# A new order of the S5 mixer's steps, the skip added on TensorE, lags in the output's PSUM bank, three buffers for weight products

## The chip, the cores and the metric

The kernel runs on one core of a Trainium2 chip. The metric is the device time of one execution in microseconds (us). TensorE (PE in the profile) multiplies matrices, VectorE (DVE) and ScalarE (ACT) work elementwise, GpSimd (POOL) works elementwise on SBUF only, and SyncE (SP) issues the DMAs.

## What is computed

A two-layer trunk over 512 tokens of width 1024, in float32. The change lies in the first mixer, an S5 state-space layer over 64 groups of 16 channels with 64 complex states each:

```python
u = rms_norm(h, a_norm) @ w_in
a_bar = exp(lam * dt);  b_bar = ((a_bar - 1) / lam) * b        # per group
s[t] = a_bar * s[t-1] + b_bar @ u[t]                           # complex scan over 512 tokens
y = real(c @ s) + d_skip * u
g = gelu(y);  val, gate = split(g @ w_glu)
h = h + val * sigmoid(gate)
```

After it come a gated feed-forward layer, stick-breaking attention and a second feed-forward layer. The change does not touch them.

## The kernel before

**Tiling.** Every large product is cut into a rounded high part and a residue, and three fp32r matmuls replace one (`mm3`, line 248). The 64 groups are worked through in four quarters `q`, each in two halves. Tokens are cut into 64 steps of L = 8, so the sum over the states becomes a short convolution inside a step of 8 (the "lags") and a recurrence over the 64 steps (the "states").

**Steps of a half (q, half).** Each is a method of the class `S5`, and the tuple `ORDER` (line 762) lists them by name.
- `turn`: eight PE transposes of the projected input into bank 2, one ACT copy to `u`.
- `weights`: six DVE operations (two complex products of 128x512), in the helper lines 836 and 837 (multiply) and 838 (add), to the tiles `w1`. `turn_weights`: eight transposes of `w1` into banks 3, then 2, two ACT copies to `vl`.
- `lags`: 16 small matmuls of `w1` with c. ACT copies most of the result to `ktt` (line 1198), and one DVE operation writes the last 16 columns with the skip `d_skip` added (line 1200). `turn_lags`: one transpose of `ktt`, an ACT copy to `kt`. `toeplitz`: eight DMAs of `kt` into `tz`.
- `outs`: six POOL operations and four DMAs, which fill `w2`.
- `inject`: 32 matmuls of `u` with `vl` into banks 4 and 5.
- `rotations` (once a quarter): six operations of 128x512 to the table `tab`, on DVE for q = 0 and 1, on POOL for q = 2 and 3. `states` (once a quarter): sixteen DVE operations with two scans, from banks 4 and 5 to `s`.
- `output`: 32 matmuls of `tz` and `u`, `w2` and `s` into bank 6, then a gelu on ACT in two parts. `turn_output`: eight transposes into bank 3, then `split_one` (lines 164 and 165): ACT writes the high part, DVE the residue. Bank 3 is free after the residue.

**Filler.** A plain number in `ORDER` takes that many steps of the generator `filler` (line 1376). It first projects quarters 1, 2 and 3 (16 steps each, six matmuls a step, called fills below), reads each projection on ACT (`read`), and then runs the first pass of the gated product (`first_pass`, three matmuls of 512 columns a fill). The fills left over when `ORDER` ends run after it, so a fill that is used early is missing later.

**What sets the order.** The calls run in the order of the tuple. On PE that order is kept (`manual_schedule(engines={PE})`, line 1437). On DVE, ACT, POOL and SP a planner decides at build time: it takes the instructions by the order of the program, and what is not ready by its own timeline lets later ones go first. The result is a fixed order for each queue. `START` (line 744) is an order by hand for PE, ACT and DVE in the part before, in which quarter 0 is projected.

**Buffers.** The temporaries of the complex products and of `states` on DVE are two tags, `tt1` and `tt2`, two buffers each (`tmp`, line 1148). `w1` has two buffers per part, `tab` has one. `LAG_BANKS` gives the PSUM banks of `lags` and `turn_lags`.

Of the kernel before, what the change touches and what calls it, by code (L numbers as in the profile page):

```python
# [7 lines left out]
F32 = mybir.dt.float32  # L8
# [3 lines left out]
ALU = mybir.AluOpType  # L12
PSUM = bass.MemoryType.PSUM

P = 128
T = 512
D = 1024
DC = D // P
# [676 lines left out]
def attention(e, ws, grow, r4=None):  # L695
# [31 lines left out]
L = 8  # L727
# [16 lines left out]
START = (  # L744
# [8 lines left out]
ST_BANK = 6  # L753
EXP_BANK = 7
G_BANK = 7
LAG_BANKS = ((1, 1), (3, 6), (3, 6), (3, 6))
P_BANKS = ((0, 1), (6, 0), (0, 1), (0, 1))
BC_BANKS = (4, 5, 4, 5)
X_BANKS = (2, 3, 4, 5, 6, 7, 2, 3)
GLU_POOL = (True, False)  # L760

ORDER = (
# [14 lines left out]
)  # L777


# [10 lines left out]
def flat(t):  # L790
    n = len(t.shape) - 1
    names = "abcd"[:n]
    return t.rearrange(f"p {' '.join(names)} -> p ({' '.join(names)})")
# [47 lines left out]
def cmul(*args):  # L841
    run(cmul_steps(*args))
# [18 lines left out]
class S5:  # L861
# [73 lines left out]
    def gains(self):  # L935
        e, nc = self.e, self.nc
        ps = e.bank(6)
        nc.tensor.transpose(ps[:, 0 : 2 * DC], self.nrow, e.ident[0 : 2 * DC, 0 : 2 * DC])
        self.gain = self.t([P, 2 * DC], F32, "gain")
        nc.vector.tensor_copy(self.gain, ps[:, 0 : 2 * DC])  # L940
        self.xhi, self.xlo, self.xps = [], [], []

    def turn_x(self, d):
# [184 lines left out]
    def read(self, q):  # L1128

        reg = self.reg  # L1130
        up = self.up[q] = self.t([C, 16, L, 16], F32, "up")
        for j in range(L):
            i, k = j % 4, j // 4
            pp = slice(C * k, C * k + C)
            self.nc.scalar.activation(
                up[:, :, j], reg[i][pp].rearrange("p (g h) -> p g h", h=16), AF.Copy, scale=self.r4[pp, i : i + 1])
# [14 lines left out]
    def weights(self, q, half):  # L1151

        W = [P, 4, L, 16]
        w1 = self.w1[q, half] = [self.t(W, F32, f"w1{k}", 2) for k in range(2)]
        sl = slice(8 * q + 4 * half, 8 * q + 4 * half + 4)
        gb = [g[:, :, sl].rearrange("p l q -> p q l").unsqueeze(3).broadcast_to(W) for g in (self.gre, self.gim)]
        bb = [b[:, sl].unsqueeze(2).broadcast_to(W) for b in self.b]
        cmul(self.nc.vector, self.tmp(W), w1[0], w1[1], gb, bb)
        for g in range(2):
            pp = slice(64 * g, 64 * g + 64)  # L1160
            for k in range(2):
                self.nc.scalar.copy(self.cm[half][k][pp, :, g], self.c[k][pp, sl])
# [22 lines left out]
    def lags(self, q, half):  # L1185

        e, nc = self.e, self.nc
        w1 = self.w1.pop((q, half))
        sl = slice(8 * q + 4 * half, 8 * q + 4 * half + 4)
        cm = self.cm[half]  # L1190
        ps = e.bank(LAG_BANKS[q][half])
        for k in range(2):
            for i in range(4):
                nc.tensor.matmul(
                    ps[32 * i : 32 * i + 32, 0:P], flat(cm[k][:, i]), flat(w1[k][:, i]), start=k == 0, stop=k == 1,
                    skip_group_check=True)
        ktt = self.ktt[q, half] = self.t([P, P], F32, "ktt", 2)
        nc.scalar.copy(ktt[:, 0 : P - 16], ps[:, 0 : P - 16])
        d = DC + 2 * q + half
        nc.vector.scalar_tensor_tensor(  # L1200
            out=ktt[:, P - 16 :], in0=self.eye, scalar=self.gain[:, d : d + 1], in1=ps[:, P - 16 : P], op0=ALU.mult, op1=ALU.add)

    def turn_lags(self, q, half):

        e, nc = self.e, self.nc
        ps = e.bank(LAG_BANKS[q][half])
        nc.tensor.transpose(ps[:, 0:P], self.ktt.pop((q, half)), e.ident)
# [130 lines left out]
    def store(self, d):  # L1338

        if d < 2:  # L1340
            if d == 0:
                self.p0 = self.t([P, 4, T], F32, "up")
            return [self.p0[:, 2 * d], self.p0[:, 2 * d + 1]]
        if d < 4:
            t = self.t([P, 2, T], F32, f"u{d - 1}")
            return [t[:, 0], t[:, 1]]
        if d < 6:
            v = flat(self.vl[d - 4]).rearrange("p (k t) -> p k t", k=2)
            return [v[:, 0], v[:, 1]]
        return [self.t([P, T], F32, f"w1{k}", 2) for k in range(2)]  # L1350

    def second_pass(self):

# [173 lines left out]
```

## Time and profile before

| | us |
|---|---|
| median of 3 runs (1248.27 to 1249.27) | 1249.25 |
| the profiled execution | 1248.93 |
| its span, first to last instruction | 1247.1 |
| PE busy | 1203.4 (96%) |
| DVE busy | 779.3 (62%) |
| ACT busy | 541.8 (43%) |
| POOL busy | 142.3 (11%) |

Times below are microseconds from the start of the span. "Idle before" is the time in which an engine stood still ahead of an instruction, with the instruction that released it. [...] A row of several instructions gives the time from the first start to the last end.

### The profile page before, as it was taken

The page shows a single profiled execution, that of the slowest core. Times are in us where ns is not written, and L with a number is a line of the kernel's source. Part 1 is how long each engine was busy: PE and PEld are TensorE (multiplying, and loading weights), DVE is VectorE, ACT ScalarE, POOL GpSimd, SP SyncE. Part 2 cuts the span into 40 slices and gives each one's busy share as a digit, 9 for nine tenths or more (in the row PEclk, how much of TensorE's full clock was granted, in tenths as well). Part 3 has the DMA queues.
Part 4 walks back from the last instruction along what each step waited for, and adds up shares of the span by engine and source line. Part 5 has one row for each costly group of instructions (what it writes and reads, how often), then busy time and mean ns, then how long its engine had stood idle before and what let it go on. Part 6 is the DMA issues. An engine that isn't in the chain of part 4 may idle for free. (4 is left out here: it accounts for less than half of the span.)

```text
span 1247.1 us, 17177 instructions
## 1 busy us (share of the span) xinstructions
PE 1203.4 (96%) x6815; PEld 1010.3 (81%) x6815; DVE 779.3 (62%) x1254; ACT 541.8 (43%) x869; POOL 142.3 (11%) x131
## 2 busy tenths in 40 slices
PE   7786899999999999999999999999999999999998
PEld 7776787888888888888899898776788888888887
DVE  7978644867565564333578998976776556552322
ACT  7653544344333333222448675744453433332210
POOL 3878530000000000000000000000300000000000
PEclk8899999999999999999999999999999999999999
DMA  7333232333333333333222211121233333332330
GB/s 190 98 92 89 72 99 90 97 90 101 97 89 101 101 89 92 95 96 100 90 85 69 69 58 62 52 68 35 85 101 88 98 91 96 102 102 87 125 109 34
DMA packets 162379, 111.68 MB, mean 90 GB/s; under 512 B 7452, under 2 KB 151868, under 8 KB 162236
## 3 DMA queue, kind: packets, MB, share of 16 engines
q1 hardware_dynamic: 161724, 109.55, 29.8%
q8 instruction: 53, 0.87, 0.3%
q10 hardware_dynamic: 576, 1.05, 0.2%
q14 instruction: 26, 0.21, 0.1%
HBM read 101.93 MB, written 2.10 MB: 83 GB/s over the span
## 5 line engine op out<-in xcount | busy, mean ns | idle before, releaser
L249 PE MATMUL b<-t_xhi,t_whi 128*128 128x512 f32 x864 | 337.0, 393 | 2.6 <-ACT p_w L1335 1.4
L250 PE MATMUL b<-t_xlo,t_whi 128*128 128x512 f32 x864 | 337.6, 391 | 1.4 <-DVE t_xlo L168 0.7
L251 PE MATMUL b<-t_xhi,t_wlo 128*128 128x512 f32 x864 | 337.4, 391 | 0.2 <-DVE t_wlo L130 0.2
L116 ACT CAST t_whi<-t_wraw 128x1024 fp32r<-128x1024 f32 (+1 forms) x166 | 172.5, 1040 | 367.7 <-PE b L250 242.2
L130 DVE TENSOR_TENSOR t_wlo<-t_wraw,t_whi 128x1024 fp32r<-128x1024 f32 (+1 forms) x154 | 189.3, 1230 | 155.0 <-ACT t_whi L116 154.3
L249 PEld LDWEIGHTS b<-t_xhi,t_whi 128*128 128x128 f32 x864 | 162.3, 188 | 38.0 <-ACT p_w L1335 1.9
L250 PEld LDWEIGHTS b<-t_xlo,t_whi 128*128 128x128 f32 x864 | 162.5, 188 | 36.8 <-DVE t_xlo L168 2.7
L251 PEld LDWEIGHTS b<-t_xhi,t_wlo 128*128 128x128 f32 x864 | 162.4, 188 | 34.7 <-DVE t_wlo L130 0.6
L457 PE MATMUL b<-t_whi,t_xhi 128*128 128x256 f32 x384 | 109.4, 286 | 1.4 <-ACT a_raw L469 1.3
L459 PE MATMUL b<-t_whi,t_xlo 128*128 128x256 f32 x384 | 109.3, 286 | 0.0
L458 PE MATMUL b<-t_wlo,t_xhi 128*128 128x256 f32 x384 | 109.2, 285 | 0.0
L314 DVE TENSOR_TENSOR p_fg<-b,p_rsrow 128x512 f32<-128x512 f32 x44 | 30.4, 691 | 87.0 <-PE b L251 80.6
L457 PEld LDWEIGHTS b<-t_whi,t_xhi 128*128 128x128 f32 x384 | 73.3, 191 | 1.9 <-ACT a_raw L469 1.8
L325 DVE TENSOR_TENSOR p_fv<-b,p_rsrow 128x512 f32<-128x512 f32 x44 | 30.4, 690 | 69.6 <-PE b L251 69.6
L458 PEld LDWEIGHTS b<-t_wlo,t_xhi 128*128 128x128 f32 x384 | 73.5, 191 | 0.2
L459 PEld LDWEIGHTS b<-t_whi,t_xlo 128*128 128x128 f32 x384 | 73.3, 191 | 0.2
L251 PE MATMUL b<-p_ahi,t_wlo 128*128 128x512 f32 x176 | 69.4, 394 | 0.0
L250 PE MATMUL b<-p_alo,t_whi 128*128 128x512 f32 x176 | 69.4, 394 | 0.0
L348 PE MATMUL b<-t_wlo,p_ahi 128*128 128x512 f32 x176 | 69.4, 394 | 0.0
L249 PE MATMUL b<-p_ahi,t_whi 128*128 128x512 f32 x176 | 69.4, 394 | 0.0
L347 PE MATMUL b<-t_whi,p_ahi 128*128 128x512 f32 x176 | 69.0, 392 | 0.0
L349 PE MATMUL b<-t_whi,p_alo 128*128 128x512 f32 x176 | 68.4, 388 | 0.0
(305 smaller groups left out, 1888.2 us busy)
## 6 DMA issues: line engine op xcount, KB each, us to landing
t_wraw<-in_ffn_w_up_dram SPq DMA_DIRECT2D x88, 512.0 KB
t_wraw<-in_ffn_w_down_dram SPq DMA_DIRECT2D x30, 512.0 KB
t_wraw<-in_a_w_glu_dram SPq DMA_DIRECT2D x16, 512.0 KB
t_wraw<-in_w_kv_dram SPq DMA_DIRECT2D x16, 512.0 KB
t_wraw<-in_ffn_w_down_dram SPq DMA_DIRECT2D x16, 448.0 KB
t_wraw<-in_a_w_in_dram SPq DMA_DIRECT2D x8, 512.0 KB
p_w<-p_w2d SPq DMA_DIRECT2D x32, 128.0 KB
t_wraw<-in_b_w_q_dram SPq DMA_DIRECT2D x8, 512.0 KB
```

What stands on the lines that cost most here:

```text
L116: nc.scalar.copy(hi, t)
L130: eng.tensor_tensor(out=lo, in0=t, in1=hi, op=ALU.subtract)
L249: nc.tensor.matmul(ps, whi, xhi, start=start, stop=False)
L250: nc.tensor.matmul(ps, whi, xlo, start=False, stop=False)
L251: nc.tensor.matmul(ps, wlo, xhi, start=False, stop=stop)
L314: nc.vector.tensor_tensor(out=g, in0=pg, in1=rr, op=ALU.mult)
L347: nc.tensor.matmul(pss[tb], xh, whi[:, j], start=k + j == 0, stop=False)
L348: nc.tensor.matmul(pss[tb], xh, wlo[:, j], start=False, stop=False)
L349: nc.tensor.matmul(pss[tb], xl, whi[:, j], start=False, stop=st)
L457: nc.tensor.matmul(reg[tb], xh, whi[:, j], start=st, stop=False, skip_group_check=True)
L458: nc.tensor.matmul(reg[tb], xh, wlo[:, j], start=False, stop=False, skip_group_check=True)
L459: nc.tensor.matmul(reg[tb], xl, whi[:, j], start=False, stop=k == 7, skip_group_check=True)
```

## The change

- `ORDER` is new. In each quarter both `inject` steps now come before the quarter's second `lags`, in quarters 1 to 3 before both. `states` follows at once, and the `lags`, `turn_lags` and `toeplitz` steps come after it. `rotations` moves ahead; `turn q 0` and `turn q 1` stand together for q = 1 and 2.
- The skip is added by one more matmul of 16 columns in `lags`, from a tile `skip` that POOL fills once. The DVE operation of line 1200 is gone, and one ACT copy moves all of `ktt`.
- `lags` and `turn_lags` of quarters 1 to 3 use bank 6, the output's, where the first half used bank 3.
- `w1` has three buffers per part.
- `read` reads the eight blocks of a projection bank by bank.
- In `START`, `x 5` stands after `high 3` and `p 1`.

```diff
-    "chain 5", "p 1", ..., "chain 4", "x 5", "high 3", "p 1", "sq 7", "low 3",
+    "chain 5", "p 1", ..., "chain 4", "high 3", "p 1", "x 5", "sq 7", "low 3",
...
-LAG_BANKS = ((1, 1), (3, 6), (3, 6), (3, 6))
+LAG_BANKS = ((1, 1), (6, 6), (6, 6), (6, 6))
...
+    10, "turn 0 0", 1, "weights 0 0", "weights 0 1", "rotations 0", 3, "vectors 0", "turn_weights 0 0", "lags 0 0",
+    "turn_weights 0 1", 1, "turn_lags 0 0", "turn 0 1", "outs 0 1", "inject 0 0", "inject 0 1", "states 0", "lags 0 1",
+    "weights 1 0", 1, "turn_lags 0 1", 3, "toeplitz 0 0", 1, "outs 0 0", 3, "toeplitz 0 1", 5, "turn 1 0", "turn 1 1",
+    "output 0 0", "weights 1 1", 1, "outs 1 0", "output 0 1", "rotations 1", "turn_output 0 0", "outs 1 1",
+    "turn_weights 1 0", 1, "turn_output 0 1", "turn_weights 1 1", "inject 1 0", "inject 1 1", "states 1", "lags 1 0",
+    1, "vectors 1", "turn_lags 1 0", "lags 1 1", 2, "weights 2 0", "turn_lags 1 1", "toeplitz 1 0", "toeplitz 1 1", 9,
+    "turn 2 0", "turn 2 1", "output 1 0", 2, "turn_weights 2 0", "output 1 1", "weights 2 1", "outs 2 0",
+    "turn_output 1 0", "rotations 2", 1, "turn_output 1 1", "outs 2 1", "turn_weights 2 1", "inject 2 0", "inject 2 1",
+    "states 2", "lags 2 0", 2, "vectors 2", "weights 3 0", "turn_lags 2 0", "lags 2 1", 2, "turn 3 0", "vectors 3",
+    "turn_lags 2 1", "toeplitz 2 0", "toeplitz 2 1", "turn 3 1", 6, "weights 3 1", "output 2 0", 2, "turn_weights 3 0",
+    "output 2 1", "outs 3 0", "rotations 3", 2, "turn_output 2 0", "turn_weights 3 1", "outs 3 1", "inject 3 0",
+    "inject 3 1", "states 3", 2, "turn_output 2 1", "lags 3 0", 2, "turn_lags 3 0", "lags 3 1", 4, "turn_lags 3 1",
+    "toeplitz 3 0", "toeplitz 3 1", 12, "output 3 0", 4, "turn_output 3 0", "output 3 1", 4, "turn_output 3 1",
...
+        self.skip = self.t([P, DC, 16], F32, "skip")
+        nc.gpsimd.tensor_tensor(
+            out=self.skip, in0=self.eye.unsqueeze(1).broadcast_to(K), in1=self.gain[:, DC:].unsqueeze(2).broadcast_to(K),
+            op=ALU.mult)
...
-        for j in range(L):
+        for j in (0, 4, 1, 5, 2, 6, 3, 7):
...
-        w1 = self.w1[q, half] = [self.t(W, F32, f"w1{k}", 2) for k in range(2)]
+        w1 = self.w1[q, half] = [self.t(W, F32, f"w1{k}", 3) for k in range(2)]
...
+        nc.tensor.matmul(
+            ps[:, P - 16 : P], e.ident, self.skip[:, 2 * q + half], start=False, stop=True, skip_group_check=True)
...
-        nc.scalar.copy(ktt[:, 0 : P - 16], ps[:, 0 : P - 16])
-        nc.vector.scalar_tensor_tensor(
-            out=ktt[:, P - 16 :], in0=self.eye, scalar=self.gain[:, d : d + 1], in1=ps[:, P - 16 : P], op0=ALU.mult, op1=ALU.add)
+        nc.scalar.copy(ktt, ps[:, 0:P])
```

## Rows read from the trace of the kernel before

**Rows 1.** Windows: busy us (count) of PE, PEld, DVE, ACT, POOL; granted clock; DMA.
```profile
50.00:100.00 50.00, 42.10 (x490) 38.17 (x489) 41.78 (x57) 27.37 (x63) 40.73 (x30) 0.90 0.31 80
100.00:150.00 50.00, 38.91 (x426) 32.91 (x426) 39.57 (x54) 22.25 (x47) 36.65 (x29) 0.97 0.32 87
...
200.00:250.00 50.00, 49.90 (x220) 41.33 (x221) 40.03 (x48) 19.30 (x26) 0.00 (x0) 1.00 0.32 95
```

**Rows 2.** Waits of PE, 48 to 215: waiter, releaser, total us, times, longest.
```profile
PE b L1170 <- DVE t_xlo L165: 6.9, 2, 5.5
PE b L1207 <- DVE p_ktt L1200: 3.4, 2, 2.4
PE b L1170 <- DVE p_ktt L1200: 3.0, 1, 3.0
...
PE b L1295 <- DVE p_s L1281: 1.8, 3, 1.2
```

**Rows 3.** DVE timeline: start, us, operation; weights 1 0, rotation 0, states 0 begin.
```profile
49.32 0.68 DVE L836 TENSOR_TENSOR p_tt<-b,p_b 128x512 f32<-128x512 f32 x1
...
54.87 1.58 DVE L836 TENSOR_TENSOR p_tt<-p_e16c 128x512 f32<-128x512 f32 x1
...
64.47 0.69 DVE L1267 TENSOR_TENSOR p_tt<-b,p_tab 128x512 f32<-128x512 f32 x1
```

**Rows 4.** POOL timeline, the same columns.
```profile
50.33 2.38 POOL L130 TENSOR_TENSOR t_wlo<-t_wraw,t_whi 128x1024 fp32r<-128x1024 f32 x1
...
82.45 1.27 POOL L1232 TENSOR_TENSOR p_w2d<-p_tp,p_tp 128x512 f32<-128x512 f32 x1 [5.44 <-DMA p_w<-p_w2d]
```

**Rows 5.** DVE timeline from the end of states 0.
```profile
73.88 2.79 DVE L1281 TENSOR_TENSOR p_s<-b,p_tt 64x504 f32<-64x504 f32 x4
...
78.79 0.68 DVE L836 TENSOR_TENSOR p_tt<-p_e16c 128x512 f32<-128x512 f32 x1
...
82.52 1.74 DVE L838 TENSOR_TENSOR p_tab<-p_tt,p_tt 128x512 f32<-128x512 f32 x1
84.19 0.68 DVE L165 TENSOR_TENSOR p_glo<-b,p_ghi 128x512 fp32r<-128x512 f32 x1
88.74 0.69 DVE L165 TENSOR_TENSOR p_glo<-b,p_ghi 128x512 fp32r<-128x512 f32 x1 [3.88 <-ACT p_ghi L164]
```

**Rows 6.** PE timeline, single steps between 53 and 122.
```profile
53.34 0.36 PE L1121 MATMUL b<-t_whi,t_xhi 128*128 128x256 f32 x1
...
54.01 0.28 PE L1123 MATMUL b<-t_whi,t_xlo 128*128 128x256 f32 x1
...
57.48 1.08 PE L1194 MATMUL b<-p_w,p_cm 128*32 128x128 f32 x16 [0.35 <-ACT p_kt L1209]
...
59.54 3.68 PE L1250 MATMUL b<-p_u,p_vl 128*64 128x64 f32 x64
...
80.94 0.71 PE L1309 MATMUL b<-t_ident,p_gl 64*128 64x64 f32 x8 [0.29 <-ACT p_vl L1171]
81.58 0.44 PE L1292 MATMUL b<-p_tz,p_u 128*64 128x128 f32 x4
...
84.92 1.09 PE L1170 MATMUL b<-t_ident,p_w 128*128 128x128 f32 x8 [1.37 <-DVE p_glo L165]
...
92.13 1.15 PE L1250 MATMUL b<-p_u,p_vl 128*64 128x64 f32 x32
...
118.41 1.97 PE L1170 MATMUL b<-t_ident,p_w 128*128 128x128 f32 x8 [5.45 <-DVE t_xlo L165]
```

**Rows 7.** ACT timeline: copy of a turn, four blocks of a read.
```profile
48.07 0.59 ACT L1146 COPY p_u<-b 128x512 f32<-128x512 f32 x1 [1.03 <-PE b L1145]
...
127.65 1.68 ACT L1135 ACTIVATE p_up<-b,p_r 64x256 f32<-64x256 f32 x4
```

**Rows 8.** PE timeline in the start: the transposes of x 5.
```profile
16.39 1.12 PE L947 MATMUL b<-t_ident,p_xt 128*128 128x128 f32 x4 [1.69 <-DVE p_mag L829]
```

**Rows 9.** DVE timeline in the start: the statistics.
```profile
29.73 0.16 DVE L982 TENSOR_SCALAR p_ms<-b 128x4 f32<-128x4 f32 x1 [2.63 <-PE b L981]
```

More of the change, by code (lines that the diff above doesn't have):

```diff
@@ L940, in gains @@
         nc.vector.tensor_copy(self.gain, ps[:, 0 : 2 * DC])
+        self.skip = self.t([P, DC, 16], F32, "skip")
+        K = [P, DC, 16]
+        nc.gpsimd.tensor_tensor(
+            out=self.skip, in0=self.eye.unsqueeze(1).broadcast_to(K), in1=self.gain[:, DC:].unsqueeze(2).broadcast_to(K),
+            op=ALU.mult)
         self.xhi, self.xlo, self.xps = [], [], []
@@ L1194, in lags @@
                 nc.tensor.matmul(
-                    ps[32 * i : 32 * i + 32, 0:P], flat(cm[k][:, i]), flat(w1[k][:, i]), start=k == 0, stop=k == 1,
+                    ps[32 * i : 32 * i + 32, 0:P], flat(cm[k][:, i]), flat(w1[k][:, i]), start=k == 0, stop=False,
                     skip_group_check=True)
+        nc.tensor.matmul(
+            ps[:, P - 16 : P], e.ident, self.skip[:, 2 * q + half], start=False, stop=True, skip_group_check=True)
         ktt = self.ktt[q, half] = self.t([P, P], F32, "ktt", 2)
-        nc.scalar.copy(ktt[:, 0 : P - 16], ps[:, 0 : P - 16])
-        d = DC + 2 * q + half
-        nc.vector.scalar_tensor_tensor(
-            out=ktt[:, P - 16 :], in0=self.eye, scalar=self.gain[:, d : d + 1], in1=ps[:, P - 16 : P], op0=ALU.mult, op1=ALU.add)
+        nc.scalar.copy(ktt, ps[:, 0:P])
     def turn_lags(self, q, half):
@@ L1349, in store @@
             return [v[:, 0], v[:, 1]]
-        return [self.t([P, T], F32, f"w1{k}", 2) for k in range(2)]
+        return [self.t([P, T], F32, f"w1{k}", 3) for k in range(2)]
     def second_pass(self):
```

16 rows, old and new, of tables (ORDER, START) are left out of this document.

## Prediction, made before the changed kernel was timed

> **What bounds the kernel now.** I read the windows first. From 200 us on TensorE is busy without a gap, 49.9 of 50 us, and so it stays but for the end; a change in the mixer can move the time only by what it does to TensorE's standing still before that. In the two windows from 50 to 150 us TensorE is busy 42.1 and 38.9 of 50, and the granted clock is 0.90 and 0.97 [rows 1]. So some 20 us of standing and some 7 us of half clock are all that can be won. Next, the waits of TensorE in that stretch: every large one ends at VectorE. `turn_weights` waits twice for the residue of a gelu that has to leave bank 3 (6.9 us), and three waits (3.4 and 3.0 us) are for the skip operation of line 1200 [rows 2]. Last, the timelines of VectorE and GpSimd, to see what was queued ahead of those operations. VectorE's queue is what decides here, and its order is the planner's.
>
> **The skip on TensorE.** It takes eight operations out of VectorE's queue, and with them the waits of 3.4 and 3.0 us [rows 2]: `turn_lags` then waits for ACT, which reads the bank right after the matmuls. The price is eight small matmuls on TensorE. None of that shape is in the trace; the 16 of a `lags` take 1.08 us at half clock [rows 6], about 0.04 us each at full clock, and a transpose of 128 columns 0.14 (eight in 1.09). I take 0.1 each, bounds 0.04 and 0.14: 0.6 us for the six that lie in the part that counts below. POOL's filling of `skip` lies in the start, beside VectorE's chain; I put it at nothing, 0.6 us at most if a VectorE operation has to stand aside once for it, as in [rows 3].
>
> **The start.** `p 1` (six matmuls, 0.75 us a fill, by the first and last of one [rows 6]) moves into the 1.69 us for which TensorE waits ahead of x 5 [rows 8]. VectorE waits 2.63 us for TensorE later in the start [rows 9], so a gain there reaches VectorE's chain. Those transposes took 1.12 us, at half clock. Between 0 (another wait takes it) and 2.6 us I take 1.3: the fill moved, at half clock. The new order of `read` frees bank 0 after four blocks instead of six; TensorE gains some 0.8 us, which the next part swallows.
>
> **VectorE's chain to the second injection.** This is the heart of it.
> - `rotations 0` now follows `weights 0 1`, where `weights 1 0` began at 49.32 [rows 3]; with the start's gain 48.0. Its six operations read two SBUF operands, and beside POOL they went at 1.6 us each (54.87 to 64.47, with two short skip operations among them [rows 3]) where the same operation took 0.68 while POOL stood still (78.79 [rows 5]). Now POOL's long residue at 50.33 (2.38 us [rows 4]) is in their way too: 10.2 us, to 58.2. The injections end on TensorE before that. `states 0` follows at once: 12.2 us (64.47 to 76.67 [rows 3, 5]), to 70.4 instead of 76.7. So far 6.3 us are won, and `output 0 0` hardly waits.
> - But `weights 1 0`, done by 54.87 before, now stands behind `states 0`. The third buffer of `w1` does not help: VectorE stood idle for 3.88 us at 84.9 [rows 5], when the next half's products had all inputs and free temporaries, and did not begin them ahead of `states 1`. I read this as temporaries being given out in the order of the program.
> - After `states 0` come four operations of `weights 1 0` (two slip in among the states, as before), six of `weights 1 1` and six of `rotations 1`, and `rotations 1` now also stands ahead of `turn_output 0 0` in the program. The residue of `turn_output 0 0`, for which `turn_weights 1 0` waits in bank 3, comes behind them. Before, ten operations took the 7.5 us from 76.67 to 84.19, the last of them 1.74 beside POOL [rows 5].
> - POOL had come back 5.8 us after the states' end (82.45 [rows 4]), when `output 0 0` had freed `w2`. Now it comes back at 76.2, and the first nine operations also end at 76.2 (5.8 us). So the remaining six ahead of the residue meet POOL: 6 x 1.6 = 9.6 us, and the residue 0.7. `turn_weights 1 0` begins at 86.6, or 88.2 if the last addition goes first, or 80.7 if POOL were away. TensorE has been ready since 76.5 and stands some 10 us. I take 86.6, as the trace has POOL without a pause once it is back.
> - From there: `turn_weights` and a fill at half clock, as after the wait of 5.45 us (1.97 us instead of 1.09 [rows 6]), 2.8 us; `turn_output 0 1` 0.65; its residue in bank 3, which the next `turn_weights` needs at once (ACT 0.6, residue 0.7, two starts), 1.45; `turn_weights` 0.95 and two injections 2.2 (1.15 each [rows 6]). They end at 94.7, against 93.2 before. By then the new order has run one fill less and has two `lags` and two `turn_lags` still to do: 2.3 us. **Loss so far 3.8 us.**
>
> [...]
>
> **From the second injection to the fourth.** Removed: the waits of 6.9, 3.0 and 1.8 [rows 2] and three of 0.3 to 0.7, 13.2 us together, and two stretches of half clock of 1.3 us (0.9 in `turn_weights`, 0.4 in the fill behind it) [rows 6]: 15.8 us. Added:
> - The second `lags` of each quarter follows `turn_lags` in the same bank 6 and waits for ACT's copy, as at 57.48 (0.35 [rows 6]): 3 x 0.35 = 1.05.
> - `turn 2 1` follows `turn 2 0` in bank 2 and waits for the copy of 0.59 [rows 7]: 0.7. `turn 3 0` comes one fill after the projection and waits for the last four blocks of its read (1.68 [rows 7]), 1.15; `turn 3 1` 0.3. The second fill of the third projection waits 0.8 for the same reason.
> - `turn_weights 2 0` and `3 0` wait for the last addition of products that now begin only after the states: 1.0 and 0.8.
> - `turn_output 1 1` waits 1.7 for the first half's residue, which stands behind ten operations of `weights 2 x` beside POOL (1.1 us each, from the ten of [rows 5] and those beside POOL); `turn_weights 2 1` then 1.45, and `turn_weights 3 1` 2.2. Bounds for these three: 1.0 each when nothing is ahead, 5.45 [rows 2] when a residue comes as late as once before.
> - Half clock after some of these: 1.8. Skip matmuls: 0.6.
>
> Together 13.55 us; gain 2.25. The `toeplitz` transfers and `outs` on SP have more room than before or the same; the late `toeplitz 2 1` is hidden behind `turn_weights 3 0` and `output 2 0`, and would cost 1 us if that cover went. After the fourth injection nothing waits, before or after.
>
> **Sum.** 3.8 - 2.25 = 1.55 us slower than the profiled 1248.93 (span 1247.1 and 1.8 around it), so 1250.5; that execution lay 0.3 under the median shown, so **1250.8**.
>
> **Rivals.**
> - **The residue gets past the rotation.** If the planner's order has the residue of `turn_output 0 0` ahead of `rotations 1`, `turn_weights 1 0` begins at 78.0, 8.6 us sooner, and the clock does not fall (1.2). `rotations 1` then ends at 88.4 and `states 1` starts 3.5 us after its injection, which costs 1.7 of wait at `output 1 0`. 1242.7. For it: residues were taken in between other operations before, once ready. Against it: the rotation now comes first in the program.
> - **Half of the collision.** The residue slips in after the rotation's first half, or POOL returns late, or the third buffer does let `weights 1 0` go ahead of `states 0` (states end at 75.4, then ten operations as before: 83.6). 3 to 6 us less: 1245 to 1249, likeliest 1247.5.
> - **The clock, slower.** The clock fell to 0.5 after waits of 5.45 us, and the injections after one of 2.4 took 3.68 us for 64 matmuls where 32 take 1.15 [rows 2, 6]; it did not fall after 1.37 (`turn_weights` 1.09 [rows 6]). The new order has five waits of 1.15 to 2.2 us close together in quarters 1 and 2. If each of four brings a fall of 1.4 instead of the 1.8 in all that I counted, that is 3.8 more: 1254.6. [...]
>
> **Chances.** About 0.2% (2.5 us) is what a measurement here tells from no change. Forecast 0.38, own range 1249 to 1253.2 (0.23 within, 0.15 slower); half of the collision 0.22 (0.08 faster, 0.14 within); residue first 0.22, 1240.5 to 1245 (faster); clock 0.18, 1253.2 to 1257.5 (slower). Faster 0.30, within 0.37, slower 0.33. The range leaves about a tenth out at each end: 1242.5 to 1256.
>
> **What would show it.** Right: `states 0` ends near 70, the residue of `turn_output 0 0` runs after `rotations 1`, whose operations take 1.5 us or more, and `turn_weights 1 0` waits about 10 us for line 165; no wait is for `ktt` on VectorE; short waits for ACT's copies ahead of `turn 2 1` and the second `lags`. Wrong: a wait there under 3 us, products of `weights 1 0` ahead of `states 0`, or `output` waiting for `states` by more than 3 us, which would mean that VectorE's chain is longer than laid out.

## The result: 11.6 us slower, most of it by TensorE's clock

The changed kernel took 1260.82 us (1259.17 to 1262.11), the kernel before 1249.26 us beside it: a ratio of 1.0095, interval 1.0079 to 1.0111. The prediction was 1250.8 with a range to 1256.0. It was wrong.

The windows of the changed kernel, in the columns of [rows 1]:

```profile
50.00:100.00 50.00, 40.34 (x449) 36.09 (x442) 40.13 (x55) 27.04 (x62) 37.06 (x30) 0.83 0.31 82
100.00:150.00 50.00, 39.86 (x375) 34.32 (x374) 35.41 (x47) 19.07 (x40) 35.06 (x28) 0.80 0.28 74
150.00:200.00 50.00, 46.96 (x379) 37.65 (x376) 13.73 (x21) 22.12 (x37) 16.62 (x9) 0.97 0.31 86
200.00:250.00 50.00, 48.56 (x214) 39.74 (x213) 32.93 (x39) 18.91 (x26) 0.00 (x0) 1.00 0.30 94
```

From 50 to 150 us TensorE is busy for 80.2 us, where it was 81.0: it hardly stands longer. But the granted clock there is 0.83 and 0.80 instead of 0.90 and 0.97. By windows of 1 us from 50 to 165 us it is 1.00 (full) or 0.50 (half) in both traces, but for the windows in which it changes. With these two levels a mean of 0.83 over 50 us is 17 us at the lower one, and 0.80 is 20. That makes 37 us, against 13 before.

To compare kernels exactly I take a place that all of them have: a matmul of `first_pass` that waits 1.44 us for a copy on ACT. Rows of PE's timeline, before and after:

```profile
200.10 0.50 PE L249 MATMUL b<-t_xhi,t_whi 128*128 128x512 f32 x1 [1.44 <-ACT p_w L1335]
```

```profile
211.42 0.50 PE L249 MATMUL b<-t_xhi,t_whi 128*128 128x512 f32 x1 [1.44 <-ACT p_w L1338]
```

11.3 of the 12.3 us of difference in span (1247.1 and 1259.4) have arisen by then. Up to this place I summed over windows of 1 us what TensorE stood (window minus busy) and what it lost to the clock (busy, times one minus the granted clock); the rest is the work as it would take at full clock. Ends of matmuls are modelled, so a microsecond of it means little.

| kernel | place, us | standing | lost to the clock | work at full clock |
|---|---|---|---|---|
| before | 200.1 | 32.1 | 12.3 | 155.7 |
| after | 211.4 | 33.4 | 20.0 | 158.0 |
| after, old order (e1) | 201.1 | 29.8 | 12.4 | 158.8 |
| after, `dec` in two buffers (e2) | 205.6 | 33.1 | 13.9 | 158.6 |
| e2, two pauses filled (e10) | 201.1 | 27.1 | 11.7 | 162.4 |
| e2, nine places filled (e5) | 197.3 | 17.8 | 3.9 | 175.6 |
| e1 with `dec` in two buffers, filled (e11) | 191.9 | 21.0 | 2.1 | 168.9 |

Before against after: 7.7 us more are lost to the clock, 1.3 us more is stood, and 2.3 us more is work, of which eight skip matmuls at 0.24 us (below) make 1.9. In the first 50 us, ahead of the new order, 4.5 us were lost to the clock before and 1.9 after (point 6 below), so from 50 us on it is 7.8 against 18.1. The injections show where. Between the second and the fourth, TensorE stood 13.2 us before and 14.8 after, and lost 3.0 us to the clock before and 12.3 after. Beyond the fourth the clock is full in both (1.00 in every window of 1 us from 156 us on before and from 164 on after, up to the place).

What TensorE waits for between 48 and 215 us, as in [rows 2]:

```profile
PE b L1198 <- ACT p_kt L1212: 7.0, 3, 5.4
PE b L1174 <- DVE t_xlo L165: 4.1, 2, 2.7
PE b L1174 <- DVE p_glo L165: 4.1, 2, 2.7
PE b L1125 <- ACT p_up L1139: 2.7, 2, 1.9
PE b L1312 <- DVE t_xlo L165: 1.8, 1, 1.8
```

The waits for the skip operation are gone, the largest wait for a residue fell from 5.5 to 2.7 us, and `lags` now waits for ACT, 5.4 us of it at one place. Steps of PE's timeline:

```profile
80.66 1.25 PE L1174 MATMUL b<-t_ident,p_w 128*128 128x128 f32 x8 [2.68 <-DVE p_glo L165]
...
85.64 1.97 PE L1174 MATMUL b<-t_ident,p_w 128*128 128x128 f32 x8 [1.40 <-DVE p_glo L165]
87.54 3.68 PE L1253 MATMUL b<-p_u,p_vl 128*64 128x64 f32 x64
...
126.33 0.40 PE L1201 MATMUL b<-p_skip,t_ident 128*128 128x16 f32 x2
126.57 0.36 PE L1125 MATMUL b<-t_whi,t_xhi 128*128 128x256 f32 x1
...
128.18 0.27 PE L1210 MATMUL b<-t_ident,p_ktt 128*128 128x128 f32 x1
133.85 1.08 PE L1198 MATMUL b<-p_w,p_cm 128*32 128x128 f32 x16 [5.40 <-ACT p_kt L1212]
...
138.95 1.11 PE L1149 MATMUL b<-t_ident,p_up 64*128 64x64 f32 x8 [0.73 <-ACT p_up L1139]
```

After two pauses of 2.68 and 1.40 us, 3.6 us apart, the second injection takes 3.68 us for 64 matmuls where 32 had taken 1.15 [rows 6]; the granted clock is 0.50 in every window of 1 us from 82 to 91 us. After the pause of 5.40 comes another of 0.73, and by windows of 3 us the lower clock (0.50) lasts from about 132.7 to 146.3 us (columns: busy of PE, granted clock, DMA):

```profile
132.00:135.00 3.00, 1.15 (x17) 0.61 0.01 3
135.00:138.00 3.00, 3.00 (x11) 0.50 0.18 41
...
144.00:147.00 3.00, 3.00 (x10) 0.61 0.32 82
```

ACT's timeline explains the wait of 5.40:

```profile
127.29 0.27 ACT L1204 COPY p_ktt<-b 128x128 f32<-128x128 f32 x1
131.07 0.62 ACT L1262 COPY p_dec<-p_mag 128x512 f32<-128x512 f32 x1 [3.52 <-DVE b L1274]
131.60 1.91 ACT L1139 ACTIVATE p_up<-b,p_r 64x256 f32<-64x256 f32 x4
133.54 0.27 ACT L1212 COPY p_kt<-b 128x128 f32<-128x128 f32 x1
```

The planner put the decay copy of the fourth quarter (line 1262) early into ACT's queue. `dec` has one buffer, so the copy stands 3.52 us until the scan of `states 2` has read the old one. Behind it are four blocks of a read and the copy of `kt`, whose source was ready at 128.45, and in bank 6 behind that copy is the next `lags`. ACT did nothing else meanwhile. So the copy of `kt` ran at 133.54, 5.1 us after its source was ready, behind all that stood ahead of it.

### The profile page after: what moved, and what is told of

It reads as the page before. It is cut to its first block, busy times and chain, and to the rows that moved or that the text cites. A ratio compares the mean times of both kernels' runs of the same rounds, so it can differ in the third digit from the quotient of the medians.

```text
span 1259.4 us, 17204 instructions
## 1 busy us (share of the span) xinstructions
PE 1214.7 (96%) x6831; PEld 1019.0 (81%) x6831; DVE 776.2 (62%) x1246; ACT 544.4 (43%) x869; POOL 140.4 (11%) x132
## 3 DMA queue, kind: packets, MB, share of 16 engines
q10 hardware_dynamic: 576, 1.05, 0.2%
## 5 line engine op out<-in xcount | busy, mean ns | idle before, releaser
L249 PEld LDWEIGHTS b<-t_xhi,t_whi 128*128 128x128 f32 x864 | 162.4, 188 | 38.4 <-ACT p_w L1338 1.9
```

What stands on the lines that cost most here:

```text
L249: nc.tensor.matmul(ps, whi, xhi, start=start, stop=False)
```

## Experiments

Theory A: the new order's pauses of TensorE, short and close together, hold its clock at the lower level. Theory B: ScalarE's queue, by the one wait of 5.4 us. Rival C: the order isn't the cause, but the skip matmul, the start or the buffers.

### Is it the order? (e1, e9, e12, e6, e7)

**e1** puts back the old `ORDER` and `LAG_BANKS` and keeps all else.

```
-LAG_BANKS = ((1, 1), (6, 6), (6, 6), (6, 6))
+LAG_BANKS = ((1, 1), (3, 6), (3, 6), (3, 6))
...
-    10, "turn 0 0", 1, "weights 0 0", "weights 0 1", "rotations 0", 3, "vectors 0", "turn_weights 0 0", "lags 0 0",
+    10, "turn 0 0", 1, "weights 0 0", "weights 0 1", 3, "vectors 0", "turn_weights 0 0", "lags 0 0", "weights 1 0",
...
```

> The changed kernel with the order of the mixer's steps and the banks of the lags as they were before; start, reading order, skip on TensorE and third buffer stay changed. Theory A (the new order leaves short pauses of TensorE before the injections and so keeps its clock low): the order is what costs, and this kernel is below the kernel before by the skip's two waits and the earlier start: 1241 to 1247 us, granted clock from 50 to 150 us at 0.93 or more. Theory B (ScalarE's queue: a kt copy behind the decay copy, 5.4 us at one place of the new order): the same side, as that place is in the new order: 1241 to 1247 us. Rival C (the skip on TensorE or the changed start is what costs): 1257 to 1262 us.

1244.26 us, ratio 0.9978 (0.9965 to 0.9992). The order of the steps, with the banks that go with it, is what costs: 16.6 us between the medians, 14.6 by the ratios; the rest of the change gains a little. Its profiled execution was the slowest of ten (1249.71), with the clock at 0.93 and 0.90 from 50 to 150 us, so the expected clock wasn't seen in it. Even against this execution the changed kernel is 10.3 us behind at the place of the table, and 7.6 us of that are lost to the clock.

**e9** gives the weights two buffers again.

```
-        w1 = ... [self.t(W, F32, f"w1{k}", 3) for k in range(2)]
+        w1 = ... [self.t(W, F32, f"w1{k}", 2) for k in range(2)]
```

> The changed kernel with two buffers for w1, as before, in place of three; the instructions of every engine stay in the same order. The prediction held the third buffer for useless, since the products tt1 and tt2 are handed out in the order of the program: no change, 1259 to 1262.5 us. If the third buffer lets weights q+1 start earlier or moves a transfer: 1 us or more to either side.

1260.40 us, ratio 1.0097 (1.0082 to 1.0112). The third buffer does nothing.

**e12** puts the skip back on VectorE, in the new order.

```
-        nc.tensor.matmul(
-            ps[:, P - 16 : P], e.ident, self.skip[:, 2 * q + half], start=False, stop=True, skip_group_check=True)
...
-        nc.scalar.copy(ktt, ps[:, 0:P])
+        nc.scalar.copy(ktt[:, 0 : P - 16], ps[:, 0 : P - 16])
...
+        nc.vector.scalar_tensor_tensor(
+            out=ktt[:, P - 16 :], in0=self.eye, scalar=self.gain[:, d : d + 1], in1=ps[:, P - 16 : P], op0=ALU.mult, op1=ALU.add)
```

> The changed kernel with the skip added on VectorE, as before. In the new order states 1, 2 and 3 stand right ahead of the lags, so the addition queues behind work of about 12 us on VectorE. If the prediction's price for it holds (3.4 and 3.0 us of waits in the whole mixer): 1264 to 1269 us. If each addition waits for the states before it: 1275 us or more. If the planner of VectorE's order slips it in between: 1260 to 1264 us.

1261.11 us, ratio 1.0113 (1.0083 to 1.0144): no difference from the changed kernel that can be told. The additions slip in between the states on VectorE. The waits of TensorE:

```profile
PE b L1206 <- DVE p_ktt L1199: 5.0, 4, 2.8
```

So 5.0 us of waits come back and cost nothing that can be seen. **e6** is the other half, the same lines the other way round: the kernel before with only the skip on TensorE.

> The kernel before with the skip added by TensorE alone. The prediction took away waits of 3.4 and 3.0 us and asked 0.1 us for each added matmul. If the skip carries the gain that the changed kernel has under the old order (4.0 us): 1243 to 1245.5 us. If its waits only move to the states, to the copies on ScalarE and to the bank of turn_weights 2 1 (2.4 us there in that run): 1246.5 to 1248.5 us.

1247.71 us, ratio 0.9995 (0.9984 to 1.0005). Two of its waits, against [rows 2]:

```profile
PE b L1299 <- DVE p_s L1285: 5.9, 4, 4.6
...
PE b L1175 <- ACT p_ktt L1205: 2.2, 1, 2.2
```

The wait of 3.0 us for the skip is one of 2.2 us for ACT's copy out of the same bank, and `output` now waits 5.9 us for the states, where it was 1.8: TensorE arrives earlier and VectorE doesn't.

**e7** is the kernel before with the changed start and read order.

```
-    ... "chain 4", "x 5", "high 3", "p 1", "sq 7", "low 3",
+    ... "chain 4", "high 3", "p 1", "x 5", "sq 7", "low 3",
...
-        for j in range(L):
+        for j in (0, 4, 1, 5, 2, 6, 3, 7):
```

> The kernel before with the changed start (the place of one transposed tile and of one high half) and the changed order of the eight read blocks alone. The prediction gave it 1.3 us (0 to 2.6). If it carries the gain under the old order: 1244 to 1246 us; by the prediction: 1246.5 to 1247.5 us; if a pause on TensorE moves and the clock takes it back: 1248 to 1249.5 us.

1248.54 us, ratio 0.9998 (0.9988 to 1.0008): no difference that can be told. Rival C falls: none of its parts shows a cost.

### ScalarE's queue (e2, e4)

**e2:**

```
-        dec = self.t(K, F32, "dec")
+        dec = self.t(K, F32, "dec", 2)
```

> The changed kernel with two buffers for the decay tile dec, so that its fourth copy on ScalarE no longer waits for the scan of states 2. Theory B (the kt copy behind that copy and four read blocks is one cause of its own): the wait of 5.4 us before lags 2 1 falls to about 1.3 us (the reads then end at 129.5 us), 4 us less, and if a pause of 1.3 us doesn't lower the clock another 5 us of the stretch at half clock behind it: 1250 to 1257 us. Theory A (short pauses anywhere hold the clock low): 4 us less and the clock stays at half behind the shorter pause: 1256 to 1258 us. Rival C (start or skip): 1260 to 1261 us, no change.

1254.80 us, ratio 1.0055 (1.0035 to 1.0076), 6.0 us less between the medians. Nothing else moved on any engine but that copy and POOL's `memset` of the tile. ACT's timeline at the place:

```profile
127.19 0.27 ACT L1204 COPY p_ktt<-b 128x128 f32<-128x128 f32 x1
128.24 1.92 ACT L1139 ACTIVATE p_up<-b,p_r 64x256 f32<-64x256 f32 x4 [0.78 <-PE b L1127]
130.18 0.27 ACT L1212 COPY p_kt<-b 128x128 f32<-128x128 f32 x1
```

The wait before `lags 2 1` is 2.1 us instead of 5.4. From the end of the third injection to the wait ahead of `turn_weights 3 1` (125.7 to 156.8 us, in e2 125.4 to 151.1) e2 takes 5.5 us less: it stands 2.3 us less, loses 3.8 us less to the clock, and has 0.7 us more work. The table's sums differ by 0.3 and 6.1 us because of other differences ahead of this stretch, in which e2 stands 1.8 us more and loses 2.0 us less; the edit does not explain those. Behind the shorter wait the clock still fell, but for 3.4 us (136.3 to 139.7, by windows of 1 us) instead of 14. So neither theory's expectation came as written: B is right about the place, and most of its price is paid through A.

**e4** undoes only the change of the lags' banks.

```
-LAG_BANKS = ((1, 1), (6, 6), (6, 6), (6, 6))
+LAG_BANKS = ((1, 1), (3, 6), (3, 6), (3, 6))
```

> The changed kernel with banks 3 and 6 for the two lags of a pair from the second pair on, as before, instead of bank 6 for both: lags 2 1 no longer waits for the kt copy out of bank 6. If the bank is the cause: the wait of 5.4 us goes, 1253 to 1256 us. Theory B (ScalarE's queue is the cause, the bank only shows it): lags 2 1 and two blocks of project run in the gap, then turn 3 0 waits for the read blocks behind the decay copy until about 133.5 us; 1.5 to 2.5 us come back: 1257 to 1260 us. Theory A: as B, and the clock falls at the same place.

1262.52 us, ratio 1.0122 (1.0104 to 1.0140). Going back to bank 3 wins nothing. The wait of 5.4 us became this one, since bank 3 is also where `vectors 2` is turned, and VectorE copies it out between the states:

```profile
PE b L1210 <- DVE t_vb L1471: 6.2, 1, 6.2
```

### The clock (e3, e10, e5)

These runs add matmuls whose results nobody uses, just ahead of a step that waits. No wait gets shorter; TensorE is only kept at work.

```
+    def idle(self, n):
+        ps = self.e.bank(2)
+        for _ in range(n):
+            self.nc.tensor.matmul(ps[:, 0:256], self.xhi[0][:, 0:P], self.xhi[0][:, 0:256], start=True, stop=True)
...
+    ... "outs 1 1", "idle 19", "turn_weights 1 0", 1, "turn_output 0 1", "idle 9", "turn_weights 1 1", ...
```

**e3** fills eight places of the changed kernel, the two above and

```
+    "idle 13" behind "turn_lags 0 1", "idle 8" ahead of "lags 1 1", "idle 12" ahead of "turn_output 1 1",
+    "idle 9" ahead of "turn_weights 2 1", "idle 40" ahead of "lags 2 1", "idle 19" ahead of "turn_weights 3 1"
```

> The changed kernel with extra matmuls on TensorE (128x256, results used by nobody, into bank 2) in eight pauses between 57 and 160 us: 13 after turn_lags 0 1, 19 and 9 before turn_weights 1 0 and 1 1, 8 before lags 1 1, 12 and 9 before turn_output 1 1 and turn_weights 2 1, 40 before lags 2 1, 19 before turn_weights 3 1, each at about 0.12 us and so a little shorter than the pause it fills. Nothing waits less. Theory A (pauses lower the clock): the clock from 50 to 150 us rises from 0.82 to 0.97 or more and 10 to 13 us come back: 1248 to 1251 us. If not the pauses but the thin matmuls of the injections lower it: the clock stays under 0.88 and the time at 1258 to 1262 us. Theory B with the clock of no weight: 1260 to 1261 us.

1250.85 us, ratio 1.0039 (1.0014 to 1.0064): 10 us come back between the medians. Two of its ten executions did not show it (1261.42 and 1262.60, mean granted clock 0.988 against 0.992 to 0.994 in the others). It is not a clean test. With these steps in the program the planner put the reads and the `kt` copy ahead of the decay copy, so that this run has e2's gain too, and the block of 40 (5.03 us) ahead of `lags 2 1` outlasted its pause.

**e10** is clean: e2 with the two pauses of the diff above filled, ScalarE's order that of e2.

> The changed kernel with two buffers for dec, and extra matmuls in two pauses only, 19 ahead of turn_weights 1 0 (pause of 3.2 us in the run without them) and 9 ahead of turn_weights 1 1 (1.40 us); the order of ScalarE's instructions is that of the run with dec alone. There TensorE had 0.50 to 0.65 of its clock from 80 to 90 us. Theory A (the pauses lower the clock): the second injection takes 2.1 us in place of 3.7, the transposes beside it 1.1 in place of 2.0, and 3.5 to 5 us come back of 1254.8 us: 1249.5 to 1251.5 us. Rival (the thin matmuls of the injection, 64 columns wide, lower it): 1254 to 1256 us, the injection again at 3.7 us.

1252.38 us, ratio 1.0040 (1.0020 to 1.0060). In the stretch itself the profiled executions answer plainly. Windows of e2 and of e10 (busy of PE, granted clock, DMA):

```profile
80.00:85.00 5.00, 3.74 (x21) 0.50 0.37 83
85.00:90.00 5.00, 4.86 (x84) 0.65 0.01 2
```

```profile
80.00:85.00 5.00, 4.65 (x40) 1.00 0.37 82
85.00:90.00 5.00, 4.34 (x92) 1.00 0.01 3
```

And the steps of e10 on PE:

```profile
80.24 1.09 PE L1174 MATMUL b<-t_ident,p_w 128*128 128x128 f32 x8 [0.21 <-DVE p_glo L165]
...
84.09 1.09 PE L1174 MATMUL b<-t_ident,p_w 128*128 128x128 f32 x8
85.11 2.08 PE L1253 MATMUL b<-p_u,p_vl 128*64 128x64 f32 x64
```

In e2 the clock fell to 0.50 at 78.3 us, in the pause, 9 us ahead of the injection's narrow matmuls, and rose while they ran (they took 2.73 us there, 3.68 in the changed kernel). With the pauses ahead of them filled they run in 2.08 us at full clock, so here the pauses and not the narrow matmuls lower the clock. By the end of the second injection e10 is 2.6 us ahead of e2 (87.1 against 89.7 us). In the whole time it is 2.4 us between the medians, less than the 3.5 to 5 expected, and the intervals of e2 and e10 overlap. The profiled execution of e10 was the fastest of ten (1249.98), so its row in the table is better than e10 as a rule; the ten go up to 1261.96 us, with a mean granted clock from 0.990 down to 0.985.

**e5** is e2 with those eight places filled, shorter ahead of `lags 2 1`, and one more ahead of `turn 3 0`.

```
-    "idle 40", "lags 2 1", 2, "turn 3 0",
+    "idle 16", "lags 2 1", 2, "idle 9", "turn 3 0",
```

> The changed kernel with two buffers for dec and with the extra matmuls of the run that fills the pauses, but 16 before lags 2 1 and 9 before turn 3 0 in place of 40 before lags 2 1 (a block of 5.0 us there that outlasted its pause). If the clock and ScalarE's queue are two causes that add up: the 2.9 us of extra matmuls saved there come off the 1250.85 us of that run, 1246.5 to 1249 us, clock at 0.97 or more from 50 to 150 us. If the double buffer only gave what the filled pause had given (one cause): 1250 to 1252 us. If there is a third cause in the new order: above 1250 us at full clock.

1245.73 us, ratio 0.9980 (0.9970 to 0.9989), 15.1 us under the changed kernel, below the expectation and below the kernel before. The clock is 0.97 and 1.00 from 50 to 150 us, and 16.1 us less are lost to it than in the changed kernel (table). Against e2 the time is 9.1 us shorter, by work that does nothing.

### Does the old order pay too? (e8, e11)

**e8** fills five pauses of e1.

```
+    "idle 14" behind "turn_lags 0 1", "idle 28" ahead of "output 0 0", "idle 42" ahead of "turn_weights 2 0",
+    "idle 16" ahead of "turn_weights 2 1", "idle 9" ahead of "turn_weights 3 1"
```

> The changed kernel under the old order and banks of the lags, with extra matmuls (128x256, unused, into bank 2) in five pauses: 14 after turn_lags 0 1, 28 before output 0 0, 42 before turn_weights 2 0, 16 before turn_weights 2 1, 9 before turn_weights 3 1. Nothing waits less. Theory A (pauses lower the clock, in either order): the clock from 50 to 150 us rises from 0.92 to 0.98 or more and 3 to 6 us come back of 1244.3 us: 1238.5 to 1241.5 us, under both kernels. Rival (the extra matmuls only take the place of idle time): 1243.5 to 1246 us.

1244.97 us, ratio 0.9971 (0.9959 to 0.9984): no gain over e1. The clock rose as expected, to 0.97 and 1.00 from 50 to 150 us, but the expected 3 to 6 us did not come. The fill after `turn_lags 0 1` ran 1.92 us and the wait of 2.0 us behind it was still there, and the 28 ahead of `output 0 0` took 3.62 us. **e11** leaves out the first, halves the second, and gives `dec` two buffers.

```
-    "idle 14" behind "turn_lags 0 1", "idle 28" ahead of "output 0 0", "idle 42" ahead of "turn_weights 2 0", "idle 16" ahead of "turn_weights 2 1"
+    "idle 14" ahead of "output 0 0", "idle 40" ahead of "turn_weights 2 0", "idle 14" ahead of "turn_weights 2 1"
...
-        dec = self.t(K, F32, "dec")
+        dec = self.t(K, F32, "dec", 2)
```

> The changed kernel under the old order and banks of the lags, with two buffers for dec and smaller fills than in the run before: none after turn_lags 0 1, 14 before output 0 0, 40 before turn_weights 2 0, 14 before turn_weights 2 1, 9 before turn_weights 3 1. Theory A: the run with 14 and 28 at the first two places lost 2 to 3 us there by filling longer than the pause lasts, and those come off its 1245.0 us: 1241 to 1243.5 us, under both kernels. Rival (under the old order the clock has nothing left to give): 1244 to 1246 us.

1240.98 us, ratio 0.9941 (0.9926 to 0.9956). It beats both kernels. The smaller fills and the second buffer were not tried apart here. Its windows:

```profile
50.00:100.00 50.00, 42.54 (x513) 38.59 (x513) 41.84 (x55) 28.65 (x64) 41.35 (x34) 1.00 0.34 88
100.00:150.00 50.00, 47.70 (x537) 41.37 (x538) 34.88 (x46) 24.59 (x50) 38.66 (x28) 1.00 0.34 90
```

With the clock nearly full, standing and work together are 189.9 us under the old order (e11) and 193.4 under the new (e5), by the table; in both some fills outlast their pause. Nothing here shows the new order to be the better one even at full clock.

## Why the prediction was wrong

1. **The step that failed is the half clock in the part on the second to the fourth injection.** The forecast took two stretches of 1.3 us away and added 1.8 for "half clock after some of these", so 0.8 us less than before. Measured there: 3.0 us lost before, 12.3 after, 9.3 more. The 1.8 us are little more than one fall. The changed kernel has four, at 95, 119, 133 and 160 us, which lose 1.7, 2.8, 5.8 and 1.7 us. The longest is one in which a further pause (0.73 us) comes before the clock has risen again, and it lasts 14 us. The same is seen once ahead of this part: the lower level lasts 10 us from 81.5 on, with the pause of 1.40 us inside it, and loses 4.1 us up to the injection's end where 1.3 were counted. The rival on the clock had the mechanism, the place and four falls, but at 1.4 us each less than half of the price. e10 bears it out for one place: with the two pauses for bank 3 filled, the clock there is 1.00 in every window of 1 us from 70 to 90 us. No run shows a length of pause from which the clock falls: around the same 1.40 us it fell in the kernel before and stayed at 1.00 in e1 (last section).
2. **The standing in that part was closer.** The standing of 13.2 us to be removed was there. The forecast put 11.2 us in its place, and 14.8 were measured. The term for the `kt` copies (3 x 0.35 = 1.05) was 7.0 us. It was priced by a row in which ACT was free; what stands ahead of that copy in ACT's queue was never looked up. Nor did every large wait of TensorE end at VectorE, as the prediction has it: two for ACT's reads of a projection came to 2.5 us, 1.8 the longer. The decay copy waits for the scan already in the kernel before, where nothing behind it was ready yet:

```profile
99.46 0.62 ACT L1259 COPY p_dec<-p_mag 128x512 f32<-128x512 f32 x1 [2.42 <-DVE b L1271]
```

3. **The skip.** That its waits go was right. That they are worth 6.4 us was wrong: alone they gave 1.1 us between the medians, which can't be told from nothing (e6), and in the new order nothing (e12). The waits moved to the states and to ACT. The skip matmul of one `lags` is two passes in the trace, and the next step follows it after 0.24 us (126.33 to 126.57 above), where 0.1 was taken and 0.14 was the upper bound.
4. **The start.** A gain of 1.3 us (0 to 2.6) was given; e7 shows 0.2, with an interval from a loss of 1.0 to a gain of 1.5, which does not exclude it.
5. **VectorE's chain.** Its order came as laid out. DVE's timeline after, against [rows 3, 5]:

```profile
44.18 1.77 DVE L835 TENSOR_TENSOR p_tt<-p_e16c 128x512 f32<-128x512 f32 x1
...
55.10 0.69 DVE L1270 TENSOR_TENSOR p_tt<-b,p_tab 128x512 f32<-128x512 f32 x1
...
77.12 0.68 DVE L836 TENSOR_TENSOR p_tt<-p_e16s,p_e16c 128x512 f32<-128x512 f32 x1
77.84 1.64 DVE L837 TENSOR_TENSOR p_tab<-p_tt,p_tt 128x512 f32<-128x512 f32 x1
79.92 0.69 DVE L165 TENSOR_TENSOR p_glo<-b,p_ghi 128x512 fp32r<-128x512 f32 x1 [0.44 <-ACT p_ghi L164]
```

Rotation 0 took 10.8 us beside POOL (forecast 10.2), its operations with two SBUF inputs 1.6 us and more each, while those of the states, with a PSUM input, took 0.69 beside POOL (at 55.10, where POOL ran one of 1.56 us from 54.38); the states started at once, and the residue came behind rotation 1. But the collision of rotation 1 with POOL did not happen: only its last operation took 1.64 us, the others 0.68. POOL was back at 77.15 us, forecast 76.2:

```profile
77.15 1.77 POOL L1235 TENSOR_TENSOR p_w2d<-p_tp,p_tp 128x512 f32<-128x512 f32 x1 [5.31 <-DMA p_w<-p_w2d]
```

The chain ran 3 us earlier than forecast, as rotation 0 began at 44.2 and not at 48.0. `turn_weights 1 0` so began at 80.7, the lower bound, not at 86.6, and the second injection ended at 91.15 instead of 94.7. This step erred by 3.5 us to the slow side, and hid some of the error of the first. The three together, 10.1 us too little for the clock, 3.6 too little for standing and 3.5 too much here, come to 10.2 us; the sum was 10.0 us too low.

6. **Where those 3.8 us came from.** The first product of `weights 0 0` on VectorE, in the kernel before, in e6 (old start) and in e1 (new start):

```profile
39.34 0.68 DVE L836 TENSOR_TENSOR p_tt<-b,p_b 128x512 f32<-128x512 f32 x1
```

```profile
34.07 0.68 DVE L836 TENSOR_TENSOR p_tt<-b,p_b 128x512 f32<-128x512 f32 x1
```

```profile
39.01 0.68 DVE L836 TENSOR_TENSOR p_tt<-b,p_b 128x512 f32<-128x512 f32 x1
```

The five microseconds go with neither start. They go with the clock. Windows of the same three executions (busy of PE, granted clock, DMA):

```profile
15.00:20.00 5.00, 3.61 (x17) 0.53 1.17 189
```

```profile
15.00:20.00 5.00, 4.16 (x35) 1.00 1.21 191
```

```profile
15.00:20.00 5.00, 4.39 (x21) 0.50 0.92 124
```

Of the fourteen profiled executions, those of the kernel before and of e1 have a granted clock of 0.83 from 10 to 30 us and begin this product at 39 us; the twelve others have 0.91 (e4) or 1.00 there and begin it between 33.4 and 34.3. e1, e8 and e11 have the same steps up to their first fill, and begin it at 39.01, 33.70 and 33.44, so this is a difference between executions and not between kernels. The prediction was worked out from an execution with the late start. A sum that has a race of 1 us in it (POOL's return against the rotation) can't be read from one execution.

7. **The third buffer** was called useless, and is (e9).

Of what the prediction would have taken as proof against it, "a wait there under 3 us" came: 2.68.

## What to carry to other kernels

Cutting TensorE's long waits into more short ones did not help here by itself (the largest wait for a residue fell from 5.5 to 2.7 us, the loss to the clock rose from 12.3 to 20.0): sum, for each window, the standing and the loss to the granted clock apart, and look for pauses that follow each other before the clock is back (5.40 and 0.73 us here, 14 us at 0.50). Where a step comes to depend on a copy, read the queue of the copying engine ahead of it, and what the first entry of that queue waits for. If pauses can't be removed, matmuls that nobody uses can stand in them (9.1 us from e2 to e5); make them shorter than the pause (e8, with blocks of 1.92 and 3.62 us, gained nothing over e1). And before a sum is worked out from one profile, compare its granted clock with that of other executions.

## What the hardware showed that was not expected

Unused matmuls bought time: 9.1 us of 1254.8 with 17 us of added work (e2 to e5). And the same pause does not always lower the clock. Ahead of `turn_weights 3 1`, before and in e1:

```profile
151.70 1.86 PE L1170 MATMUL b<-t_ident,p_w 128*128 128x128 f32 x8 [1.40 <-DVE t_xlo L165]
```

```profile
154.07 1.09 PE L1175 MATMUL b<-t_ident,p_w 128*128 128x128 f32 x8 [1.40 <-DVE t_xlo L165]
```

1.40 us of waiting in both, for the same residue; the transposes behind it took 1.86 us in one and 1.09 in the other, and by windows of 1 us the granted clock was 0.50 from 152 to 155 us in one and 1.00 from 146 to 160 in the other. (Before, 0.34 us more were stood 2 us earlier.) What decides it stays open. It shows in the times: of the ten executions of e1, the seven from 1242.2 to 1245.7 us have a mean granted clock of 0.990 to 0.993, the three from 1246.9 to 1249.7 have 0.987 and 0.988. The four of e11, at 0.996 and 0.997, lie between 1240.3 and 1241.9. The clock is not all of it: the ten of e5, at 0.992 to 0.997, still spread from 1244.1 to 1248.5.
